# A decoder trunk on one core: the second gate's row requested late in the second product of the down projection, and an eviction's x tiles two steps behind its first operations

## The chip, the cores and the metric

The kernel runs on one core of one Trainium2 chip. The metric is the device time of one execution in microseconds (us). Engines are named as the profile names them: PE is TensorE (PEld its weight loads), DVE VectorE, ACT ScalarE, POOL GpSimd, SP SyncE, which here issues the DMAs (SPq is its queue of them).

## What is computed

One layer of an autoregressive trunk: a modulated RMSNorm, a mixer of three head groups, a gated residual, a second modulated RMSNorm, and a convolutional feed-forward network with a gated residual. The change lies in the last product, `w_down`, and in the gated residual `gt2` behind it. Cut to that:

```python
D_MODEL, SEQ, D_FF = 1024, 2048, 2816

def conv_ffn(h, w_up, w_conv, b_conv, w_down):
    z = h @ w_up
    z = causal_depthwise_conv(z, w_conv, b_conv)
    a, gv = jnp.split(z, 2, axis=-1)
    return (jax.nn.silu(a) * gv) @ w_down

def reference(x, c, ...):
    ...
    x = x + gt1 * y
    h = rms_norm(x, g_ffn[l]) * (1.0 + sc2) + sh2
    x = x + gt2 * conv_ffn(h, w_up[l], w_conv[l], b_conv[l], w_down[l])
    return x
```

All is float32.

## The kernel before

**The down projection.** The activations lie transposed in device memory as `act_d` (2816 x 2048), x after the mixer as `x2_d` (2048 x 1024), the two gates as `gt_d` (2 x 1024). The 2048 positions are done in two halves H of 1024. For each half the product of activations (2816 deep) and `w_down` is cut into 2 x 2 blocks and done with seven block products in place of eight, in the order 1, 2, 7, 6, 5, 4, 3. The sums and differences of blocks that this needs are made on VectorE. Each block product has a depth of 11 slices (`KH`) of 128 rows. A step of the program is one slice of one product: four groups of three matmuls, 12 in all, since each operand is split into a high and a low half to keep float32 precision (`mm3`, L54 high x high, L55, L56). So one half has 77 steps, and every step loads, prepares and multiplies one slice.

**Preparation.** `Down.prep` makes the operands of a slice. For products 1 and 2 they are an activation tile and a weight tile as loaded. For product 7 they are a difference of activations (L1649) and a difference of weight tiles (L1651: the tile `t2w`, minus the freshly loaded `wd`). L1654 and L1655 form product 6's activations. Then both operands are split: ACT copies the high half (L1670, tile `wsph`), VectorE subtracts it to get the low half (L1671, tile `wspl`). These split tiles have 12 buffers, that is three steps. The second matmul of a step is the first to need the low half of the weight tile.

**Loads.** `Down.load` requests the `act` tiles (128 x 1024, 512 KB, L1622) and the weight tiles `wd` and `t2w` (128 x 512, 256 KB, L1628) six steps ahead. `wd` has 8 buffers; a request waits on SyncE's queue until its buffer is free, and whatever is behind it on the queue waits too. The gate row `gt2` (one row of 1024 spread over 128 partitions, 512 KB into the core) is requested once, where the program reaches step `n_left`, which is slice 4 of product 1 in the first half (L2009).

**Eviction.** When a product's sum is complete, `Down.post` puts work on the list `later`; the loop takes one entry at each step. `Down.final` is the eviction of products 2, 5 and 4: per group of 128 rows it requests an x tile (tag `s`, four buffers, L1705), makes a first operation on the sum (L1719: times gate, or L1717: plus a kept sum), and in a later entry finishes (L1724, L1725) and writes the result out (L1726). Product 2 evicts while product 7 runs.

**What sets the order.** From the steps behind the first 14 on, the order of instructions on each engine is not that of the text: the framework's scheduler orders them by priority, by what is ready in its own reckoning, and by the buffers that are free. So a moved request can change the order on engines that the diff does not mention. SyncE, VectorE and ACT each do their instructions in the order that the scheduler left.

The two places in the code:

```python
        if i == n_left:                                  # L1999
            ...
            gt2 = pool.tile([P, D], F32, name="gt2")
            dma(gt2, gt_d[1:2, :].broadcast_to([P, D]))  # L2009
```

Of the kernel before, what the change touches and what calls it, by code (L numbers as in the profile page):

```python
# [33 lines left out]
def trunk(  # L34
# [307 lines left out]
    def h_load(n):  # L342

        out_ = []
        for k in range(4):
            t = b_tile(n, k)
            dma(t.bitcast(F32), hc_d[COMBO.index(n), k])
            out_.append(t)
        return out_
# [8 lines left out]
    def down_open_right():  # L358
        pool.open("dn_r", "right", ("wd", 2048, 8))
        pp.open("dn_r", "right", ("db0", 2048, 4))  # L360
# [261 lines left out]
    class Weights:  # L622
# [7 lines left out]
        def load(self, n=2):  # L630
            k = len(self.raw)
            if k == KT:
                return
            raw = pool.tile([P, 512], F32, name="wr", tag=self.tags[k])
            o = 0
            for col, wd in self.parts[:n]:
                dma(raw[:, o : o + wd], w_in[k * P : (k + 1) * P, col : col + wd])
                o += wd
            self.raw.append(raw[:, : self.width])
# [857 lines left out]
    class Group:  # L1497
# [37 lines left out]
        def prep(self, p):  # L1535
            self.sums(p)
            self.high(p)
            self.low(p)
# [70 lines left out]
    class Down:  # L1609
# [90 lines left out]
        def rest(self, ti, nl, i):  # L1700

            r = slice(self.H * 1024 + ti * 512 + i * P, self.H * 1024 + ti * 512 + i * P + P)
            ns = slice(nl * 512, nl * 512 + 512)
            xr = self.tmp("s")
            dma(xr, x2_d[r, ns])  # L1705
            return r, ns, xr

        def final(self, ti, nl, src, more=None):
            got = {}

            def load(i):
                got[i] = self.rest(ti, nl, i)

            def sum_(i):
                got["o", i] = o = self.tmp("o")
                if more:
                    V.tensor_tensor(o, src[i], more[i], op=ALU.add)  # L1717
                else:
                    V.tensor_tensor(o, src[i], gt2[:, nl * 512 : nl * 512 + 512], op=ALU.mult)  # L1719

            def rest(i):
                (r, ns, xr), o = got[i], got["o", i]
                if more:
                    V.tensor_tensor(o, o, gt2[:, ns], op=ALU.mult)  # L1724
                V.tensor_tensor(o, o, xr, op=ALU.add)  # L1725
                dma(out[r, ns], o)  # L1726

            for i in range(4):
                later.append(lambda i=i: (load(i), sum_(i)))
            for i in range(4):  # L1730
                later.append(lambda i=i: rest(i))

        def post(self, p):
# [38 lines left out]
    def down_open_left():  # L1772
        pool.open(
            "dn_l", "left", ("t2w", 2048, 11), ("s1", 2048, 4), ("u2", 2048, 4), ("o", 2048, 5), ("gt2", 4096, 1), *[("act%d" % n, 4096, 1) for n in range(12, 14)]
        )
        pp.open("dn_l", "left", ("db1", 2048, 4))


    later = []
# [22 lines left out]
    at_ = {s: i for i, s in enumerate(steps)}  # L1802
# [22 lines left out]
    def up_groups(i):  # L1825

        n = len(groups)
        if n < len(gs) and (n < 2 or last_of[gs[n - 2]] <= i):
            groups[gs[n]] = Group(*gs[n])
# [168 lines left out]
    for i, s in enumerate(steps):  # L1998
        if i < 14:  # L1999
            continue  # L2000
        if i == n_left:
            while later:
                later.pop(0)()
            pool.close("up_l")
            pool.close("zy")
            pp.close("up_l")
            down_open_left()
            gt2 = pool.tile([P, D], F32, name="gt2")
            dma(gt2, gt_d[1:2, :].broadcast_to([P, D]))  # L2009
        if i == n_open:  # L2010
            groups[s[1], s[2]].mm(s[3])
        if i == n_open:
            pp.close("up_r")
            down_open_right()
        if i >= n_open:
            while loaded < min(i + AHEAD + 3, n_left + AHEAD + 3 if i < n_left else len(steps)):
                load(loaded)
                loaded += 1
        prep(i + AHEAD)
        if i == 14:  # L2020
            written.close()
        up_groups(i + AHEAD)
        if i != n_open:
            if s[0] == "up":
                groups[s[1], s[2]].mm(s[3])
            else:
                downs[s[1]].mm(s[2], s[3])
        if i:
            q = steps[i - 1]
            if q[0] == "up":  # L2030
                groups[q[1], q[2]].post(q[3])
                if q[1:3] == (0, 21) or q[1:] == (0, 21, 3):
                    hb[1, OF[q[3]]] = h_load(OF[q[3]])
            elif q[3] == KH - 1:
                downs[q[1]].post(q[2])
        if later:
            later.pop(0)()
# [34 lines left out]
```

## Time and profile before

| what | value |
|---|---|
| runs shown | 2573.66, 2574.22, 2579.74 us; median 2574.22 |
| the profiled execution's own time | 2579.28 us |
| its span, from first to last instruction | 2577.6 us |
| granted TensorE clock in it | 0.998 |
| busy: PE, DVE, ACT | 98%, 77%, 50% of the span |
| moved by DMA | 379.57 MB, mean 147 GB/s |
| gate row issued, and first used | 2169.6, 2214.3 us |

A busy share says how full an engine is over the whole span. What a stage is worth is read from that stage's own window. Three views follow each other in the reading: windows that compare stages, an engine's instructions in order of time with what ended its waits in square brackets, and the chain of waits that ended last. A DMA's row in a timeline of SPq is its issue only; that its data has landed shows in the chain, or in who waits for it.

### The profile page before, as it was taken

How to read it: one execution, taken by the hardware profiler on the slowest of the kernel's cores; microseconds unless marked ns; L12 is line 12 of the kernel's file. 1: busy time of each engine (PE TensorE's matmuls, PEld its weight loads, DVE VectorE, ACT ScalarE, POOL GpSimd, SP SyncE). 2: the span in 40 equal slices, each digit the busy share in tenths (PEclk: the TensorE clock that was granted, in tenths of full speed). 3: DMA queues.
4: the chain of work that ended last, by engine and by line, in shares of the span. 5: the costliest groups of instructions: out<-in, count | busy, mean ns of one | idle time of the engine just before them, and what ended most of it. 6: DMA issues, size and time to landing. Idle time of an engine off the chain costs nothing.

```text
span 2577.6 us, 36355 instructions
## 1 busy us (share of the span) xinstructions
PE 2526.7 (98%) x12553; PEld 2099.4 (81%) x12569; DVE 1993.4 (77%) x3406; ACT 1281.9 (50%) x2443; POOL 404.5 (16%) x537
## 2 busy tenths in 40 slices
PE   6999999999999999999999999999999999999999
PEld 6888888888787877778878888888888887888887
DVE  7657656576388888865689888888888887997897
ACT  5443343433388788843555444444444444444443
POOL 2013310133266566510000000000000000000000
PEclk9999999999999999999999999999999999999999
DMA  7345753455654445157823222265222218567423
GB/s 261 111 124 168 220 176 95 132 161 145 181 155 132 119 127 168 54 192 233 294 82 98 89 83 82 83 219 172 90 74 88 85 66 290 184 234 264 155 86 119
DMA packets 302671, 379.57 MB, mean 147 GB/s; under 512 B 31758, under 2 KB 194412, under 8 KB 300440
## 3 DMA queue, kind: packets, MB, share of 16 engines
q1 hardware_dynamic: 302488, 377.26, 46.3%
q8 instruction: 99, 1.62, 0.3%
q14 instruction: 84, 0.69, 0.1%
HBM read 276.44 MB, written 100.74 MB: 146 GB/s over the span
## 4 chain that ended last, share of the span: by engine, by line
PE 54%; DVE 5%; DMA 4%; ACT 2%; issue 2%; POOL 1%; SPq 0%; ACTq 0%; DVEq 0%
PE ub L56 10%; PE ub L55 10%; PE ub L54 10%; PE db L55 5%; PE db L56 5%; PE db L54 5%; PE tp L259 2%; PE sp L206 2%; PE op L245 1%; PE op L246 1%; DMA ld<-y_d 1%; DMA x_d<-x 1%; DMA hc_d<-hl 1%; DMA ld<-yt_d 1%; DVE L L212 1%
## 5 line engine op out<-in xcount | busy, mean ns | idle before, releaser
L54 PE MATMUL acc<-wh,hh 128*128 128x512 f32 (+2 forms) x752 | 280.7, 374 | 1.2 <-DVE vhl L815 1.2
L54 PE MATMUL ub<-T,wsph 128*128 128x512 f32 x704 | 273.9, 389 | 1.2 <-ACT wsph L1529 1.2
L55 PE MATMUL ub<-T,wsph 128*128 128x512 f32 x704 | 274.3, 390 | 0.2 <-DVE T L1477 0.2
L56 PE MATMUL ub<-T,wspl 128*128 128x512 f32 x704 | 273.9, 389 | 0.0
L56 PE MATMUL acc<-wh,hl 128*128 128x512 f32 (+2 forms) x752 | 269.7, 361 | 0.3 <-DVE hl L606 0.2
L55 PE MATMUL acc<-wl,hh 128*128 128x512 f32 (+2 forms) x752 | 269.3, 359 | 0.6 <-DVE wl L648 0.6
L55 PE MATMUL db<-wspl,wsph 128*128 128x512 f32 x616 | 240.0, 390 | 2.6 <-DVE wspl L1671 2.4
L56 PE MATMUL db<-wsph,wspl 128*128 128x512 f32 x616 | 239.5, 389 | 0.0
L54 PE MATMUL db<-wsph 128*128 128x512 f32 x616 | 239.5, 389 | 0.0
L1529 ACT CAST wsph<-S 128x512 fp32r<-128x512 f32 x176 | 109.3, 622 | 219.3 <-PE ub L55 151.9
L263 DVE TENSOR_TENSOR plo<-tp,phi 128x512 fp32r<-128x512 f32 (+1 forms) x320 | 187.0, 607 | 30.9 <-ACT phi L262 29.0
L55 PE MATMUL ub<-B,wsph 128*128 128x512 f32 x528 | 205.7, 390 | 0.9 <-DVE B L1477 0.8
L54 PE MATMUL ub<-B,wsph 128*128 128x512 f32 x528 | 205.7, 390 | 0.0
L56 PE MATMUL ub<-B,wspl 128*128 128x512 f32 x528 | 205.5, 389 | 0.0
L223 ACT ACTIVATE L<-L,nm 128x1024 f32<-128x1024 f32 (+2 forms) x192 | 172.5, 902 | 34.8 <-DVE nm L212 32.7
L259 PE MATMUL tp<-ident,L 128*128 128x128 f32 x1088 | 177.7, 275 | 6.4 <-DVE plo L263 4.0
L262 ACT CAST phi<-tp 128x512 fp32r<-128x512 f32 (+1 forms) x320 | 159.7, 520 | 43.5 <-PE tp L259 41.8
L1670 ACT CAST wsph<-act 128x512 fp32r<-128x512 f32 x132 | 82.3, 624 | 195.1 <-PE db L55 185.0
L206 PE MATMUL sp<-kk,q 128*128 128x512 f32 (+3 forms) x640 | 170.3, 377 | 3.5 <-DVE nm L212 2.5
L228 POOL TENSOR_SCALAR L<-L,rs 128x1024 f32<-128x1024 f32 (+2 forms) x192 | 168.0, 885 | 11.0
L259 PEld LDWEIGHTS tp<-ident,L 128*128 128x128 f32 x1088 | 131.0, 141 | 37.3 <-DVE plo L263 8.5
L56 PEld LDWEIGHTS acc<-wh,hl 128*128 128x128 f32 x752 | 142.4, 190 | 22.0 <-DVE hl L606 0.7
(338 smaller groups left out, 5969.7 us busy)
## 6 DMA issues: line engine op xcount, KB each, us to landing
w<-in_w_up_dram SPq DMA_DIRECT2D x88, 512.0 KB
wd<-in_w_down_dram SPq DMA_DIRECT2D x154, 256.0 KB
wa<-in_w_ada_dram SPq DMA_DIRECT2D x96, 256.0 KB
act_d<-yc SPq DMA_DIRECT2D x44, 512.0 KB
act<-act_d SPq DMA_DIRECT2D x44, 512.0 KB
wr<-in_w_in_dram SPq DMA_DIRECT2D x64, 256.0 KB
q<-q_d SPq DMA_DIRECT2D x128, 128.0 KB
hc_d<-hl SPq DMA_DIRECT2D x28, 512.0 KB
```

Of the source, the lines that this page charges most:

```text
L54: T.matmul(ps, lh, rh, start=start, stop=False, skip_group_check=resume)
L55: T.matmul(ps, lh, rl, start=False, stop=False, skip_group_check=resume)
L56: T.matmul(ps, ll, rh, start=False, stop=stop, skip_group_check=resume)
L206: T.matmul(sp[:, b : b + bw], q2[n][:, qs], kk[:, s0 + b : s0 + b + bw], start=n == 0, stop=n == 1 and not last)
L212: V.tensor_tensor_reduce(out=L[c], in0=sp[:, :w], in1=nf[:, s0 : s0 + w], scale=-1.0, scalar=3.0e38 if c == 0 else nm[:, 0:1], op0=ALU.add ...
L223: A.activation(L[c], L[c], AF.Exp, bias=nm[:, n - 1 : n], scale=-1.0, accum_out=rs[:, c : c + 1])
L228: G.tensor_scalar(t, t, rs[:, 0:1], 1.0, op0=ALU.mult, op1=ALU.mult)
L259: T.transpose(tp[:, i * P : (i + 1) * P], rows[i][j // 8][:, (j % 8) * P : (j % 8 + 1) * P], ident)
L262: A.copy(hi[:, c0:], tp[:, c0:])
L263: V.tensor_tensor(lo[:, c0:], tp[:, c0:], hi[:, c0:].bitcast(F32), op=ALU.subtract)
L1529: A.copy(self.wa[p][0], self.source(p))
L1670: A.copy(hi, v)
```

## The change

The gate row's tile is still made at `n_left`, but its request moves to slice 9 of product 2 in the first half, 16 steps on in the program. In `final`, the request of the x tile of a group moves from the entry of the group's first operation to the entry two steps later, and where it meets a finishing entry it stands behind it. The number of entries stays at 8.

```diff
-            for i in range(4):
-                later.append(lambda i=i: (load(i), sum_(i)))
-            for i in range(4):
+            for i in range(6):
+                later.append(lambda i=i: (i < 4 and sum_(i), i > 3 and rest(i - 4), i > 1 and load(i - 2)))
+            for i in range(2, 4):
                 later.append(lambda i=i: rest(i))
...
             gt2 = pool.tile([P, D], F32, name="gt2")
+        if i == at_["dn", 0, 2, 9]:
             dma(gt2, gt_d[1:2, :].broadcast_to([P, D]))
```

No instruction is added or removed. What the scheduler makes of it shows at three places, all in the first half's products 1, 2 and 7. Elsewhere, and on PE everywhere, the order stands; ACT swaps one copy with one cast. The numbers behind the names count tiles; from the gate row on they are one or a few lower after the change, and otherwise mean the same tiles.

SyncE's queue, where the gate row stood, before:

```order
L1628 DMA wd_21962<-in_w_down_dram 128x512
L1622 DMA act_22096<-act_d_73 128x1024
L2009 DMA gt2_21814<-gt_d_71 128x1024
L1622 DMA act_21888<-act_d_73 128x1024
L1622 DMA act_21912<-act_d_73 128x1024
```

and where it stands now, with the x tiles of product 2's eviction behind it (`wd_22149`, `wd_22173`, `wd_22197` are the weight tiles of slices 0, 1, 2 of product 7, `wd_22308` and `wd_22335` of slices 6 and 7):

```order
L1628 DMA wd_22149<-in_w_down_dram 128x512
L1628 DMA t2w_22195<-in_w_down_dram 128x512
L2010 DMA gt2_21814<-gt_d_71 128x1024
L1628 DMA wd_22173<-in_w_down_dram 128x512
L1628 DMA wd_22197<-in_w_down_dram 128x512
...
L1628 DMA wd_22277<-in_w_down_dram 128x512
L1628 DMA wd_22308<-in_w_down_dram 128x512
L1628 DMA wd_22335<-in_w_down_dram 128x512
L1705 DMA s_22362<-x2_d_70 128x512
L1628 DMA wd_22364<-in_w_down_dram 128x512
```

The gate row moved 19 requests further on; it stood ahead of the activation tile of product 2's slice 1 (`act_21888`), and now stands ahead of the weight tile of product 7's slice 1. The first x tile moved behind two more weight tiles.

VectorE at the end of product 1, before (`act_21840` and `wd_21842` belong to its slice 10, `act_21864` and `wd_21866` to slice 0 of product 2, `act_21888` to slice 1):

```order
L1671 TENSOR_TENSOR wspl_21893<-act_21840,wsph_21892 128x512
L1671 TENSOR_TENSOR wspl_21897<-wd_21842,wsph_21896 128x512
L1654 TENSOR_TENSOR act_21593<-act_21593,act_21888 128x512
L1655 TENSOR_TENSOR act_21593<-act_21593 128x512
L1671 TENSOR_TENSOR wspl_21917<-act_21864,wsph_21916 128x512
L1654 TENSOR_TENSOR act_21610<-act_21610,act_21912 128x512
L1671 TENSOR_TENSOR wspl_21921<-wd_21866,wsph_21920 128x512
```

and now:

```order
L1654 TENSOR_TENSOR act_21593<-act_21593,act_21887 128x512
L1671 TENSOR_TENSOR wspl_21892<-act_21839,wsph_21891 128x512
L1655 TENSOR_TENSOR act_21593<-act_21593 128x512
L1671 TENSOR_TENSOR wspl_21896<-wd_21841,wsph_21895 128x512
L1654 TENSOR_TENSOR act_21610<-act_21610,act_21911 128x512
L1671 TENSOR_TENSOR wspl_21916<-act_21863,wsph_21915 128x512
L1655 TENSOR_TENSOR act_21610<-act_21610 128x512
L1671 TENSOR_TENSOR wspl_21920<-wd_21865,wsph_21919 128x512
```

L1654, which reads the activation tile of product 2's slice 1, moved ahead of both splits of product 1's slice 10.

VectorE in product 2, from the splits of its slice 6 to those of its slice 8, before (`wd_22022`, `wd_22048`, `wd_22074` are the weight tiles of slices 6, 7, 8; the L1651 rows are product 7's, slices 1 to 6):

```order
L1651 TENSOR_TENSOR t2w_22020<-wd_22174,t2w_22020 128x512
L1671 TENSOR_TENSOR wspl_22077<-act_22018,wsph_22076 128x512
L1671 TENSOR_TENSOR wspl_22081<-wd_22022,wsph_22080 128x512
L1651 TENSOR_TENSOR t2w_22046<-wd_22198,t2w_22046 128x512
L1651 TENSOR_TENSOR t2w_22072<-wd_22225,t2w_22072 128x512
L1671 TENSOR_TENSOR wspl_22103<-act_22044,wsph_22102 128x512
L1651 TENSOR_TENSOR t2w_22098<-wd_22252,t2w_22098 128x512
L1671 TENSOR_TENSOR wspl_22107<-wd_22048,wsph_22106 128x512
L1651 TENSOR_TENSOR t2w_22124<-wd_22277,t2w_22124 128x512
L1671 TENSOR_TENSOR wspl_22129<-act_22070,wsph_22128 128x512
L1651 TENSOR_TENSOR t2w_22148<-wd_22310,t2w_22148 128x512
L1671 TENSOR_TENSOR wspl_22133<-wd_22074,wsph_22132 128x512
```

and now, the two pieces that differ:

```order
L1651 TENSOR_TENSOR t2w_22019<-wd_22173,t2w_22019 128x512
L1651 TENSOR_TENSOR t2w_22045<-wd_22197,t2w_22045 128x512
L1671 TENSOR_TENSOR wspl_22076<-act_22017,wsph_22075 128x512
L1671 TENSOR_TENSOR wspl_22080<-wd_22021,wsph_22079 128x512
...
L1651 TENSOR_TENSOR t2w_22123<-wd_22277,t2w_22123 128x512
L1651 TENSOR_TENSOR t2w_22147<-wd_22308,t2w_22147 128x512
L1671 TENSOR_TENSOR wspl_22128<-act_22069,wsph_22127 128x512
L1651 TENSOR_TENSOR t2w_22171<-wd_22335,t2w_22171 128x512
L1671 TENSOR_TENSOR wspl_22132<-wd_22073,wsph_22131 128x512
```

Slice 2's L1651 moved ahead of the splits of product 2's slice 6, and slice 7's ahead of the weight split of its slice 8, where slice 6's stood last before.

## The prediction

> **What bounds the kernel now.** The page's busy shares come first, then the windows of the down projection, since both edits lie there and nowhere else.
>
> ```profile
> PE 2526.7 (98%) x12553; PEld 2099.4 (81%) x12569; DVE 1993.4 (77%) x3406; ACT 1281.9 (50%) x2443; POOL 404.5 (16%) x537
> ...
> core 0: us, PE busy (x) PEld busy (x) DVE busy (x) ACT busy (x) POOL busy (x), PEclk, DMA share, GB/s
> 2147.00:2220.00 73.00, 70.45 (x307) 56.97 (x306) 58.42 (x91) 33.23 (x57) 0.00 (x0) 1.00 0.84 289
> 2220.00:2565.00 345.00, 345.00 (x1524) 285.67 (x1523) 304.86 (x500) 150.60 (x266) 0.00 (x0) 1.00 0.51 170
> 2565.00:2577.60 12.60, 8.01 (x35) 6.14 (x34) 6.83 (x10) 0.72 (x2) 0.00 (x0) 0.97 0.22 83
> ```
>
> TensorE (PE) sets the end. From 2220 to 2565 it has not one idle moment, so nothing done there can save time. In 2147 to 2220, the first two products of the first half, 73.00 - 70.45 = 2.55 us are idle. That is nearly all that this change can reach; the 4.6 us after 2565 are the last eviction, which it does not touch. PE's own rows say where the idle time is:
>
> ```profile
> 2177.88 0.39 PE L55 MATMUL db<-wspl,wsph 128*128 128x512 f32 x1
> ...
> 2180.37 0.39 PE L54 MATMUL db<-wsph 128*128 128x512 f32 x1
> 2181.63 0.50 PE L55 MATMUL db<-wspl,wsph 128*128 128x512 f32 x1 [0.87 <-DVE wspl L1671]
> 2181.97 0.40 PE L56 MATMUL db<-wsph,wspl 128*128 128x512 f32 x1
> ...
> 2184.25 0.39 PE L54 MATMUL db<-wsph 128*128 128x512 f32 x1
> 2184.77 0.50 PE L55 MATMUL db<-wspl,wsph 128*128 128x512 f32 x1
> 2185.10 0.39 PE L56 MATMUL db<-wsph,wspl 128*128 128x512 f32 x1
> ...
> 2198.27 0.39 PE L54 MATMUL db<-wsph 128*128 128x512 f32 x1
> 2198.50 0.39 PE L55 MATMUL db<-wspl,wsph 128*128 128x512 f32 x1
> ...
> 2203.71 0.39 PE L54 MATMUL db<-wsph 128*128 128x512 f32 x1
> 2205.66 0.50 PE L55 MATMUL db<-wspl,wsph 128*128 128x512 f32 x1 [1.56 <-DVE wspl L1671]
> 2206.00 0.40 PE L56 MATMUL db<-wsph,wspl 128*128 128x512 f32 x1
> ```
>
> Undisturbed, a matmul starts every 345.00 / 1524 = 0.226 us, so one slice of a product, 12 matmuls, takes 2.72 us. Against that spacing the delays, each with the matmul behind it, are 1.14 us at slice 0 of the second product (2180.37), 0.39 us at slice 1 (2184.25) and 1.83 us at slice 8 (2203.71): 3.36 us, counted by starts. Each time the second matmul lacks the low half of its weight tile, which VectorE writes at L1671. The chain of waits says why VectorE is late, and its timeline shows the queue it holds:
>
> ```profile
> 2169.67 0.30 SPq L2009
> 2170.07 8.25 DMA act<-act_d
> 2189.68 5.61 DMA wd<-in_w_down_dram
> 2198.13 6.09 DMA wd<-in_w_down_dram
> ...
> 2178.35 0.69 DVE L1654 TENSOR_TENSOR act<-act 128x512 f32<-128x512 f32 x1 [4.21 <-DMA act<-act_d]
> 2180.29 0.68 DVE L1654 TENSOR_TENSOR act<-act 128x512 f32<-128x512 f32 x1
> 2180.89 0.69 DVE L1671 TENSOR_TENSOR wspl<-wd,wsph 128x512 fp32r<-128x512 f32 x1
> ...
> 2193.30 0.69 DVE L1651 TENSOR_TENSOR t2w<-wd,t2w 128x512 f32<-128x512 f32 x1 [3.65 <-DMA wd<-in_w_down_dram]
> 2197.12 0.68 DVE L1651 TENSOR_TENSOR t2w<-wd,t2w 128x512 f32<-128x512 f32 x1
> 2202.91 0.69 DVE L1651 TENSOR_TENSOR t2w<-wd,t2w 128x512 f32<-128x512 f32 x1 [2.12 <-DMA wd<-in_w_down_dram]
> 2204.92 0.69 DVE L1671 TENSOR_TENSOR wspl<-wd,wsph 128x512 fp32r<-128x512 f32 x1
> ```
>
> VectorE stands in the preparation of later products (L1654 for product 6, L1651 for product 7), waiting for a transfer, and the splits that PE needs next are behind it. The first wait goes back to an activation tile requested right after the gate row (SPq L2009). So the gate row really is on the path at the first delay. The third delay has nothing of it: x tiles and wd tiles are in flight there.
>
> **The change part by part.** First, the gate row leaves 2169.6. What it held up is read from SyncE's queue and from the DMA windows:
>
> ```profile
> SPq L1628 <- DMA gt<-gt_d: 1.6, 1, 1.6
> ...
> 2176.55 0.33 SPq L1628 DMA_DIRECT2D wd<-in_w_down_dram  x1
> 2194.02 1.53 SPq L1628 DMA_DIRECT2D wd<-in_w_down_dram  x2
> ...
> 2170.00:2182.00 12.00, 11.13 (x50) 8.91 (x49) 6.21 (x10) 6.46 (x14) 0.00 (x0) 1.00 1.00 333
> 2186.00:2194.00 8.00, 8.00 (x37) 6.60 (x36) 4.35 (x9) 3.43 (x6) 0.00 (x0) 1.00 0.97 334
> 2194.00:2195.00 1.00, 1.00 (x6) 0.84 (x5) 1.00 (x2) 0.00 (x0) 0.00 (x0) 1.00 0.41 154
> ```
>
> The queue's 1.6 us wait for the gate row ends at 2176.5: the row landed then, 1.8 us before the activation tile behind it (2170.07 + 8.25 = 2178.3). The engines are full (share 1.00) and serve in order here, so the activation tile takes the gate's place and lands at 2176.5. Unchanged VectorE order would save slices 0 and 1 their 1.14 + 0.39 = 1.53 us. But the order changes: L1654 now stands ahead of the split of slice 10 of the first product. Starts on VectorE are 0.60 us apart (2180.29, 2180.89), so L1654 at 2176.5 is followed by the act split at 2177.1, L1655 at 2177.7 and the wd split at 2178.3, done at 2179.0. PE wants it at 2177.88: a new delay of 1.1, with the matmul behind it 1.2 us. The next slices follow without a wait (wd split of slice 0 at 2180.7, done at 2181.4, wanted at 2181.7). Net: -1.53 + 1.2 = -0.3 us. Bounds: the new delay is 0 if the tile lands as fast as the wd tile (2169.6 + 5.61 = 2175.2), and 3.1 us if it lands at 2178.35 as before. I take 1.2, by the gate's own landing.
>
> Second, the gate row is now requested ahead of the wd tile for slice 1 of product 7, which was issued at 2189.68 and landed 5.61 us later at 2195.3. Its 524,288 bytes take 1.57 us at 334 GB/s, so slice 1 lands at 2196.9. Slice 2 is issued when L1651 of slice 0 has freed a buffer (2193.30 + 0.69, issued 2194.02), and was used at 2197.12, so it takes 3.1 us or less. The engines had 0.59 us of free time in 2194 to 2195; the gate's bytes fill that, and the rest falls on slice 2: between 2197.1 and 2198.7, I take 2197.7. In the new VectorE order both L1651, of slices 1 and 2, stand ahead of the split of slice 6 of the second product. That gives L1651 at 2197.7, the act split at 2198.3, the wd split at 2198.9, done at 2199.6. PE, 0.3 us earlier than before, wants it at 2198.2 instead of 2198.50: a delay of 1.45 us. At slice 8 the wd split now waits for L1651 of slice 7, formerly slice 6. Slice 7's request leaves when slice 3's L1651 (at 2199.5, next after that split) has freed its buffer, at 2200.2, and no longer has two x tiles ahead of it; at 3.1 us plus part of a tile I have it at 2203.8, L1651 at 2204.2, the split at 2204.8, done at 2205.5, where PE at 2199.65 + 2 x 2.72 = 2205.1 waits 0.4 us. The old delay at slice 8, 1.83 us, is replaced by 1.45 + 0.4 = 1.85. Bounds: 0 if slice 2 lands before 2196.3, and 6.3 us if every landing takes the longest measured 6.09 us (worked out with the rivals).
>
> Third, the consumers of the late tiles:
>
> ```profile
> L1719 DVE TENSOR_TENSOR o<-db,gt x8: 681/684/684, 2214.3 to 2427.4; 128x512 f32<-128x512 f32 x8
> L1725 DVE TENSOR_TENSOR o<-o,s x24: 681/684/687, 2222.1 to 2553.4; 128x512 f32<-128x512 f32 x24
> L1705 SPq DMA_DIRECT2D s<-x_d x32: 319/423/1588, 2197.6 to 2527.8; - x32
> ```
>
> The gate is first used at 2214.3. Requested near 2189 and landing after even 8.25 us, it has 17 us to spare. Of the 32 x requests only four change place on SyncE's queue; the first left at 2197.6 and is used at 2222.1, and at 2200.5 it still has some 15 us after 6.09 us of transfer. So both edits cost nothing by lateness; what hides it is PE's work on six further slices. Without that cover each would cost its whole landing, 6 to 8 us.
>
> The sum against the profiled execution's span, 2577.6 us: -1.53 + 1.2 - 1.83 + 1.85 = -0.3 us. The profiled execution took 2579.28 us, 5.1 us above the median of the three runs shown, 2574.22; the terms are differences, so I take them from the median: 2573.9 us.
>
> **The rivals.** B, short landings: with the gate gone the tiles come soon enough that VectorE never keeps PE waiting; all 3.36 us go, and the time is 2570.9 us. For it speaks the second half, which has the same products and no gate row:
>
> ```profile
> 2355.00:2425.00 70.00, 70.00 (x311) 57.95 (x310) 52.45 (x84) 31.69 (x56) 0.00 (x0) 1.00 0.57 187
> ```
>
> PE does not wait there at all. Against it: the engines are busy to 0.57 there and to 0.84 in 2147 to 2220. The Trainium skill, "SBUF — State Buffer", section "The DMA setup-cost knee", would give this rival: it has a transfer take about 2 us plus its bytes at 436 GB/s, an estimate of 2.6 us for a wd tile and 3.2 us for an activation tile. The trace does not agree in this stretch, with 5.61, 6.09 and 8.25 us, since requests queue behind each other.
>
> C, the slower side: L1651 of slice 2 holds VectorE until its tile has landed, with slice 6's split behind it. If that takes the longest time measured for such a tile, 2194.02 + 6.09 = 2200.1, the wd split starts at 2201.3 and is done at 2202.0: 3.8 us late. Slice 7 of product 7, requested when slice 3's L1651 is through near 2202.6, lands at 2208.7, and the split is done at 2210.0 where PE at 2202.0 + 2 x 2.72 = 2207.45 waits 2.5 us. Together 6.3 in place of 1.83, with -0.3: +4.2, so 2578.4 us. It decides as soon as slice 2 lands after about 2198.0; from there each us late is a us of PE. With the first bound too (3.1 for 1.2) it is +6.1, 2580.3 us.
>
> D, the change does less than it says: the gate row is named late in the second product, but the queue has it only some 20 requests further on, while that product's first slices run, and the buffers decide most of the rest. Then the delays only change places: 2574.2 us.
>
> **How the numbers follow.** My forecast, near 2573.9, has 0.45; B 0.22; C 0.25; D 0.08. All four lie within 0.3% of 2574.22 (7.7 us), about what a measurement of this kernel can tell from no change. The range reaches from B, with half a us for its rounding, to C with part of the first bound: 2570.4 to 2580.0. The run spread before, 2573.66 to 2579.74, fits in it. Faster by over 0.3% would need more than the idle time there is, so 0.03, for runs that scatter. Slower by over 0.3% needs C's worst and more, or scatter: 0.10. Within: 0.87.
>
> **What would show it.** The gate's issue moves from 2169.6 to about 2189 and L1654's first wait ends near 2176.5. PE's delays stand at slice 10 of the first product and at slices 6 and 8 of the second, not at slices 0 and 1. If all are gone, B is right; if L1651's wait ahead of slice 6 is over 2 us longer than I have it, C. PE idle after 2220, or L1719 or L1725 waiting for a DMA, would prove the third part wrong, and a change over 7.7 us the whole.

## The result, and the profile after

| | before, in the same runs | after the change |
|---|---|---|
| median of 17 runs each | 2575.5 us (2572.84 to 2581.36) | 2580.45 us (2577.44 to 2582.59) |
| ratio, 95% interval | | 1.0015 [1.0009, 1.0022] |
| profiled execution: time, span, clock | 2579.28, 2577.6, 0.998 | 2578.68, 2576.7, 0.997 |

The change makes the kernel slower by 0.15%, 0.0015 x 2575.5 = 3.9 us (2.3 to 5.7 by the interval). That is less than 0.3%, but the interval does not reach 1. The two medians are 4.95 us apart; this text goes by the ratio, which has the interval. The two profiled spans can't be subtracted: in the profile of before, what lies ahead happened to run later. The first matmul of product 1's slice 10 starts 3.43 us later there than after the change, where it starts at 2174.22:

```profile
2177.65 0.39 PE L54 MATMUL db<-wsph 128*128 128x512 f32 x1
```

So the stage is compared with itself, and a time of the changed kernel "in the frame of before" is that time plus 3.43 us. The windows of the changed kernel, columns as before:

```profile
2147.00:2220.00 73.00, 69.91 (x294) 55.49 (x293) 57.45 (x89) 33.19 (x56) 0.00 (x0) 0.98 0.79 277
2206.00:2208.00 2.00, 2.00 (x6) 1.56 (x7) 2.00 (x4) 0.00 (x0) 0.00 (x0) 0.59 0.99 363
2208.00:2210.00 2.00, 2.00 (x7) 1.57 (x6) 2.00 (x4) 0.00 (x0) 0.00 (x0) 0.56 1.00 364
2220.00:2565.00 345.00, 345.00 (x1524) 285.65 (x1523) 303.16 (x498) 151.10 (x266) 0.00 (x0) 1.00 0.52 170
```

PE is still without a gap from 2220 on. In the stage of the change it is idle for 73.00 - 69.91 = 3.09 us, where it was 2.55, and for some 3.6 us it has another loss that idle time does not show: the granted clock (the column behind the engines) is 0.59 and 0.56, and only 6 or 7 matmuls start in 2 us, where nearly 9 fit. PE's rows show both:

```profile
2174.22 0.39 PE L54 MATMUL db<-wsph 128*128 128x512 f32 x1
2175.14 0.50 PE L55 MATMUL db<-wspl,wsph 128*128 128x512 f32 x1 [0.54 <-DVE wspl L1671]
...
2194.09 0.39 PE L54 MATMUL db<-wsph 128*128 128x512 f32 x1
2194.68 0.50 PE L55 MATMUL db<-wspl,wsph 128*128 128x512 f32 x1 [0.20 <-DVE wspl L1671]
...
2197.33 0.39 PE L54 MATMUL db<-wsph 128*128 128x512 f32 x1
2198.09 0.50 PE L55 MATMUL db<-wspl,wsph 128*128 128x512 f32 x1 [0.38 <-DVE wspl L1671]
...
2203.77 0.39 PE L54 MATMUL db<-wsph 128*128 128x512 f32 x1
2205.92 0.50 PE L55 MATMUL db<-wspl,wsph 128*128 128x512 f32 x1 [1.76 <-DVE wspl L1671]
...
2206.60 0.63 PE L54 MATMUL db<-wsph 128*128 128x512 f32 x1
2207.03 0.63 PE L55 MATMUL db<-wspl,wsph 128*128 128x512 f32 x1
```

These are slice 10 of product 1 and slices 6, 7 and 9 of product 2. Each time the second matmul of a slice lacks the low half of its weight tile, as before, but at other slices. Against the undisturbed spacing of 0.226 us the delays, each with the matmul behind it, are 0.80, 0.46, 0.64 and 2.03 us (and 0.24 at slice 8). Slices 0 and 1 have none now. Behind the longest, seven matmuls in a row start 0.43 us after the one ahead of them; with the shorter steps at both ends that adds 1.6 us.

The chain of waits and VectorE's timeline say what VectorE stood at:

```profile
2166.16 6.41 DMA act<-act_d
...
2198.36 6.19 DMA wd<-in_w_down_dram
```

```profile
2172.59 0.69 DVE L1654 TENSOR_TENSOR act<-act 128x512 f32<-128x512 f32 x1 [4.62 <-DMA act<-act_d]
2173.20 0.69 DVE L1671 TENSOR_TENSOR wspl<-act,wsph 128x512 fp32r<-128x512 f32 x1
2173.80 0.69 DVE L1655 TENSOR_TENSOR act<-act 128x512 f32<-128x512 f32 x1
2174.41 0.68 DVE L1671 TENSOR_TENSOR wspl<-wd,wsph 128x512 fp32r<-128x512 f32 x1
...
2191.85 0.69 DVE L1651 TENSOR_TENSOR t2w<-wd,t2w 128x512 f32<-128x512 f32 x1 [0.72 <-DMA wd<-in_w_down_dram]
2192.73 0.69 DVE L1651 TENSOR_TENSOR t2w<-wd,t2w 128x512 f32<-128x512 f32 x1 [0.19 <-DMA wd<-in_w_down_dram]
...
2203.23 0.69 DVE L1651 TENSOR_TENSOR t2w<-wd,t2w 128x512 f32<-128x512 f32 x1 [2.18 <-DMA wd<-in_w_down_dram]
2203.84 0.68 DVE L1671 TENSOR_TENSOR wspl<-act,wsph 128x512 fp32r<-128x512 f32 x1
2204.57 0.69 DVE L1651 TENSOR_TENSOR t2w<-wd,t2w 128x512 f32<-128x512 f32 x1
2205.18 0.68 DVE L1671 TENSOR_TENSOR wspl<-wd,wsph 128x512 fp32r<-128x512 f32 x1
```

First, L1654 waits 4.62 us for the activation tile of slice 1 of product 2, and the weight split of slice 10 (2174.41) stands third behind it. Last, L1651 of slice 8 of product 7 waits 2.18 us, and between it and the weight split of slice 9 (2205.18) stands L1651 of slice 9 too. SyncE's queue has the weight tiles of those two slices between the x tiles:

```profile
2184.15 0.44 SPq L2010 DMA_DIRECT2D gt<-gt_d  x1
...
2196.56 0.43 SPq L1705 DMA_DIRECT2D s<-x_d  x1
2197.47 0.33 SPq L1628 DMA_DIRECT2D wd<-in_w_down_dram  x1
2197.84 0.42 SPq L1705 DMA_DIRECT2D s<-x_d  x1
2198.36 0.38 SPq L1628 DMA_DIRECT2D wd<-in_w_down_dram  x1
```

Before, the first x tile stood two weight tiles earlier, between those of slices 5 and 6. The wait of 2.12 us at 2202.91 there was slice 5's L1651, the one behind it slice 6's, and the split that came too late was that of slice 8. Now they are slices 8 and 9, and the split is that of slice 9.

The order of VectorE in the section on the change stops at the splits of slice 8. Behind them it differs too. Before, slice 8's L1651 (2206.93) stood between the two splits of slice 9, and slice 9's (2208.28) behind both:

```profile
2205.59 0.69 DVE L1651 TENSOR_TENSOR t2w<-wd,t2w 128x512 f32<-128x512 f32 x1
2206.20 0.68 DVE L1671 TENSOR_TENSOR wspl<-act,wsph 128x512 fp32r<-128x512 f32 x1
2206.93 0.69 DVE L1651 TENSOR_TENSOR t2w<-wd,t2w 128x512 f32<-128x512 f32 x1
2207.54 0.68 DVE L1671 TENSOR_TENSOR wspl<-wd,wsph 128x512 fp32r<-128x512 f32 x1
2208.28 0.69 DVE L1651 TENSOR_TENSOR t2w<-wd,t2w 128x512 f32<-128x512 f32 x1
```

Now both stand one place further ahead, as the rows from 2203.23 to 2205.18 show. So slice 9's weight split now waits for the tiles of slices 8 and 9, where it waited for those of slices 7 and 8.

### The profile page after: what moved, and what is told of

Read it like the earlier page. It is cut to its first block, busy times and chain, and to the rows that moved or that the text cites. A ratio compares the mean times of both kernels' runs of the same rounds, so it can differ in the third digit from the quotient of the medians.

```text
span 2576.7 us, 36369 instructions
## 1 busy us (share of the span) xinstructions
PE 2528.1 (98%) x12569; PEld 2099.3 (81%) x12569; DVE 1993.7 (77%) x3406; ACT 1282.7 (50%) x2443; POOL 406.3 (16%) x537
## 4 chain that ended last, share of the span: by engine, by line
PE 53%; DVE 5%; DMA 5%; ACT 2%; issue 2%; POOL 1%; SPq 0%; ACTq 0%; DVEq 0%
PE ub L56 10%; PE ub L55 10%; PE ub L54 10%; PE db L55 5%; PE db L56 5%; PE db L54 5%; PE tp L259 2%; PE sp L206 2%; PE op L245 1%; PE op L246 1%; DMA ld<-y_d 1%; DMA ld<-yt_d 1%; DMA x_d<-x 1%; DMA hc_d<-hl 1%; DVE L L212 1%
```

## The experiments

Fifteen runs, 11 timed executions each, in four groups; every ratio is against the kernel before in the same group on the same chip (medians there 2575.98, 2576.25, 2576.51 and 2573.63 us). The theories named in the expectations: O says that the moved order on VectorE is the cause, since an instruction that waits for a tile holds up the splits behind it. G says that it is the bytes of the gate row at their new place, X that it is the x tiles at theirs. P came last: that the late requests are worth something by themselves, hidden by the order.

Delays of PE are sums of start-to-start times beyond 0.226 us over both products, half-speed matmuls included, from the one profiled execution of each run. With the original two profiles:

| kernel | ratio, 95% interval | delays, us | where (p1, p2: product; slice) |
|---|---|---|---|
| before, profile shown | | 3.65 | p2: 0, 1, 8 |
| before again | 0.9994 [0.9985, 1.0002] | 2.41 | p2: 0, 1, 7 to 10 |
| after | 1.0015 [1.0009, 1.0022] | 6.48 | p1: 5, 10; p2: 6 to 9; half speed |
| after again | 1.0015 [1.0006, 1.0024] | 3.94 | p1: 10; p2: 6 to 9 |
| gate row late alone | 1.0010 [1.0001, 1.0019] | 4.08 | p1: 10; p2: 6, 8 to 10 |
| x tiles late alone | 1.0005 [0.9996, 1.0014] | 2.85 | p2: 0, 1, 8, 9 |
| no gate row | 1.0008 [0.9999, 1.0017] | 5.75 | p1: 5, 10; half speed; p2: 9 |
| changed requests, old VectorE order | 0.9998 [0.9989, 1.0007] | 1.05 | p2: 7, 9, 10 |
| changed, L1654 alone put back | 1.0003 [0.9994, 1.0012] | 1.98 | p2: 9 |
| changed, L1651 alone put back | 1.0004 [0.9995, 1.0013] | 2.13 | p2: 7, 9 |
| changed, both held later | 0.9988 [0.9979, 0.9997] | 0.00 | |
| the same, repeated | 0.9992 [0.9983, 1.0001] | 0.00 | |
| gate row late, both held later | 0.9991 [0.9982, 1.0000] | 0.11 | |
| kernel before, both held later | 0.9990 [0.9981, 0.9999] | 0.49 | p1: 5, 6 |
| x tiles late, both held later | 0.9995 [0.9986, 1.0004] | 0.00 | |
| written order, requests of before | 1.0003 [0.9994, 1.0012] | 2.16 | p2: 0, behind ACT |
| written order, changed requests | 1.0004 [0.9994, 1.0013] | 1.76 | p2: 0, behind ACT |

**The two kernels as they are.** No edit.

> The kernel before once more, for a second profile: both theories have the delays at slices 0, 1 and 8 of product 2 again, 2.5 to 4 us in sum, and a ratio to before of 1 within its interval. Half-speed matmuls in this stretch here too would mean that they are not the change's alone.

> The changed kernel once more, for a second profile and a second timing. Both theories: +3 to +5 us against before; PE delays at slice 10 of product 1 and slices 6 to 9 of product 2, 4 to 5 us in sum. If the half-speed matmuls behind slice 9 belong to these delays and not to one execution, they are there again, some 2 us more.

The change's 1.0015 came again. In the repeat there is no stretch of low clock, though the wait at slice 9 is nearly as long:

```profile
2203.91 0.39 PE L54 MATMUL db<-wsph 128*128 128x512 f32 x1
2205.84 0.50 PE L55 MATMUL db<-wspl,wsph 128*128 128x512 f32 x1 [1.54 <-DVE wspl L1671]
```

So the half speed is an extra of some executions. The repeat of before had 0.4 and 0.34 us at slices 0 and 1 of product 2, not the 1.14 and 0.39 us from which the prediction worked, and at slice 8 0.4 in place of 1.83. Slices 7, 9 and 10, which had lost nothing, lost 0.2, 0.5 and 0.5. One profiled execution had sized these terms. The sum, 2.41, is just below the 2.5 to 4 expected.

**One part of the change alone.** The two hunks of the change, each by itself: the gate row's request at slice 9 of product 2, and the x tiles two entries later.

> The gate row is requested at slice 9 of product 2 as in the change; the x tiles are requested as before. Theory G (the gate row's new place ahead of the wd tiles of product 7, with two L1651 ahead of slice 6's splits, is what costs): PE delays at slice 10 of product 1 near 0.8 us and at slices 6 and 7 of product 2 near 0.5 us each, as in the changed kernel, and the old delay of 1.8 us at slice 8, since the x tiles stand where they stood; delays 1 us or more above before's 3.4 us in sum, time +2 to +5 us against before. Theory X (the x tiles' new place costs): delays at slices 0 and 1 gone, nothing new but 0.8 us at slice 10, time -1 to 0 us.

> The x tiles are requested two steps behind the first operations; the gate row is requested as before. Theory G: the delay of 1.8 us at slice 8 of product 2 moves to slice 9 with about its old length, the delays of 1.5 us at slices 0 and 1 stay; time within 1.5 us of before. Theory X: the delay at slices 8 and 9 grows by 2 us or more, time +2 to +5 us.

The parts also part the order. The gate row alone moves L1654 and slice 2's L1651 ahead, as in the change; the x tiles alone move slice 7's L1651, and behind it those of slices 8 to 10, one place ahead. With the gate row alone the delay at slice 10 of product 1 is 1.19 us and that at slice 6 is 1.64; slice 8 has 0.76, where G had expected the old 1.8. With the x tiles alone, slices 0 and 1 keep theirs (0.70 and 0.40), and the delay of slice 8 turns up at slice 9, with the same cause:

```profile
2203.71 0.39 PE L54 MATMUL db<-wsph 128*128 128x512 f32 x1
2205.24 0.50 PE L55 MATMUL db<-wspl,wsph 128*128 128x512 f32 x1 [1.14 <-DVE wspl L1671]
```

By time the gate row's part is clear of 1 and that of the x tiles can't be told from nothing; but the two intervals overlap, so the shares stay open.

**No gate row at all.** The gate's tile is filled with ones on GpSimd, so the last residual leaves its second gate out, and the row is not requested at all. The x tiles stay early in the text; on SyncE's queue two of them leave earlier than before, behind the weight tiles of slices 2 and 3, and two behind those of slices 7 and 8. VectorE's order in products 1 and 2 comes out as in the change.

```diff
-            dma(gt2, gt_d[1:2, :].broadcast_to([P, D]))
+            G.memset(gt2, 1.0)
```

> The gate row is not loaded: its tile is filled with ones on GpSimd, so the second gate is left out of the result; x tiles as before. It bounds what any place for the gate row can bring. Theory G: the delays at slices 0, 1 of product 2 (1.5 us) fall to 0.5 or less and none is new at slices 6 and 7; slice 8 keeps its delay or loses up to 1.8 us; time -1 to -3.4 us against before. Theory X says the same of the gate row, so this run sizes the gate's share for both.

By time it lies between the two kernels, and the interval parts it from neither; G had expected it 1 to 3.4 us below before. By the trace, the delay at slice 10 does not need the gate row. Without a byte of it L1654 waits longer than before, since in the new order VectorE comes to it earlier, with both of slice 10's splits still to do:

```profile
2170.40 0.69 DVE L1671 TENSOR_TENSOR wspl<-wd,wsph 128x512 fp32r<-128x512 f32 x1
2177.00 0.69 DVE L1654 TENSOR_TENSOR act<-act 128x512 f32<-128x512 f32 x1 [5.91 <-DMA act<-act_d]
2177.61 0.69 DVE L1671 TENSOR_TENSOR wspl<-act,wsph 128x512 fp32r<-128x512 f32 x1
2178.21 0.69 DVE L1655 TENSOR_TENSOR act<-act 128x512 f32<-128x512 f32 x1
2178.81 0.69 DVE L1671 TENSOR_TENSOR wspl<-wd,wsph 128x512 fp32r<-128x512 f32 x1
```

The delay at slice 10 is 2.10 us, the longest seen there, and half speed follows it (the granted clock is the third number from the right):

```profile
2178.00:2180.00 2.00, 0.45 (x2) 0.40 (x3) 2.00 (x4) 0.44 (x1) 0.00 (x0) 1.00 0.78 298
2180.00:2182.00 2.00, 2.00 (x7) 1.57 (x6) 2.00 (x5) 1.08 (x2) 0.00 (x0) 0.58 0.71 239
2182.00:2184.00 2.00, 2.00 (x6) 1.54 (x6) 2.00 (x4) 1.04 (x3) 0.00 (x0) 0.57 0.72 225
```

Slices 6 and 7 have no delay here, as G expected. But the delay at slice 10 and the half speed behind it bring PE there some 3.6 us later, which leaves VectorE that much more time, so this run does not decide between G and O at these two slices. Slice 9 has 1.60 us.

**The changed requests in the old order.** L1654 and L1651 of the first half are held behind those splits behind which they stood before the change (`issue_after` only orders instructions on one engine; it adds no wait for data). PE's work is the change's, and SyncE's requests too, but for one swap of an activation and a weight tile. VectorE's order is that of before, but for the weight split of product 2's slice 1, which stays one place earlier, as in the change. In all kernels with holds the line numbers go up: L1651 is L1654 there, L1654 is L1659, and the split L1671 is L1676.

```diff
+                after = {1: (2, 5, 1), 2: (2, 6, 1), 6: (2, 8, 0), 7: (2, 8, 1), 8: (2, 9, 0), 9: (2, 9, 1), 10: (2, 10, 0)}.get(k)
+                with tc.issue_after(self.split_[after]) if after and self.H == 0 else ExitStack():
-                V.tensor_tensor(bv, B[0], bv, op=ALU.subtract)
+                    V.tensor_tensor(bv, B[0], bv, op=ALU.subtract)
...
+                after = {1: (1, 10, 1), 2: (2, 0, 0)}.get(k)
+                with tc.issue_after(self.split_[after]) if after and self.H == 0 else ExitStack():
-                V.tensor_tensor(a(2, 1), a(2, 1), a(2, 2), op=ALU.add)
+                    V.tensor_tensor(a(2, 1), a(2, 1), a(2, 2), op=ALU.add)
```

A key (2, 5, 1) means product 2, slice 5, weight tile; 0 is the activation tile.

> All requests of the changed kernel, but L1654 and L1651 are held behind the splits that stood ahead of them before the change. Theory O (the new order on VectorE costs, since a wait for a tile stands ahead of splits that PE needs sooner; the gate row's transfer costs little): the delay at slice 10 of product 1 is gone or moves to slice 0 of product 2 with under 0.8 us, those at slices 6 and 7 fall under 0.3 us each; delays at least 1 us less in sum than in the changed kernel, time -1 to +1.5 us against before. Theory G (the gate row's bytes ahead of product 7's tiles cost): slices 6 to 9 keep 2 us or more of delay, time +2 to +5 us.

This is the run that decides: late requests, old order, and the loss is gone (0.9998). Against the change's 1.0015 only the order differs, up to that swap. The reverse, the new order with all the old requests, was not run; the kernel without the gate row comes nearest to it, and its time settles nothing.

**Written order.** The stretch from `n_left` to slice 2 of product 7 in the order of the text, with the requests of before and of the change.

```diff
+            written.enter_context(tc.manual_schedule())
+        if i == at_["dn", 0, 7, 2]:
+            written.close()
+        if i == n_left:
```

> The kernel before with the order of the text, on every engine, from slice 4 of product 1 to slice 2 of product 7 in the first half: no L1654 and no L1651 stands ahead of a split that PE needs sooner. The gate row is requested at slice 4 of product 1. Theory O: no PE delay over 0.5 us in product 2, time -1 to -4 us against before. Theory G: the gate row ahead of the activation tile still delays the start of product 2 by 0.8 us or more; the rest is gone.

> The changed kernel with the order of the text over the same steps. Theory O: the same as written_before within 1 us, since without waits ahead of the splits neither place of the gate row is felt. Theory G: 1.5 us or more slower than written_before, with delays at slices 6 to 9 of product 2.

Ratios 1.0003 [0.9994, 1.0012] and 1.0004 [0.9994, 1.0013]: where the scheduler has no say, early and late requests take the same time, which again speaks against G and X. O had expected 1 to 4 us less than before here and no delay over 0.5 us in product 2, and missed both. As a test of O it says less, since the text's order brings a wait of its own, for the copies that empty product 1's sums:

```profile
2179.21 0.39 PE L56 MATMUL db<-wsph,wspl 128*128 128x512 f32 x1
2181.49 0.50 PE L54 MATMUL db<-wsph 128*128 128x512 f32 x1 [1.89 <-ACT s L1697]
```

**One hold at a time.** The two holds of the old order, each alone; the diff is one of the two pieces above.

> The changed kernel with one thing put back: L1654 (product 6's activations) stands on VectorE where it stood before the change, behind the splits of slice 10 of product 1; L1651 stays in the change's order. O (VectorE's order is the cause, in two places): the delay at slice 10 of product 1 (0.57 and 0.80 us in the two profiles of the changed kernel) goes, those at slices 6 to 9 of product 2 stay at 2 to 3.5 us together; ratio 1.0005 to 1.0012. If L1651's order is the whole cause: as the changed kernel, 1.0015. Rival G (the bytes of the gate row at their new place): 1.0015 too, with the delay at slice 10 still there.

> The changed kernel with the other thing put back: L1651 (product 7's weight differences) stands on VectorE where it stood before the change; L1654 stays in the change's order. O: the delay at slice 10 of product 1 stays at 0.5 to 1.2 us, those at slices 6 to 9 of product 2 fall from 2.9 to 3.4 us to 0.8 to 2; ratio 1.0002 to 1.0009. If L1654's order is the whole cause: 1.0015, with L1651's part at nothing. Rival G: 1.0015, the delays at slices 6 to 9 unchanged.

With L1654 put back the delay at slice 10 is gone and slice 9 keeps 1.89 us; with L1651 put back slices 7 and 9 have 1.00 and 1.12, together just above the 0.8 to 2 expected. Slice 9's 1.12 is there though only slice 8's L1651, which waits 1.73 us, stands between its two splits; so putting the order back takes away only a part of that delay, while a late tile still costs the rest. Each brings the ratio down by about 0.0011, both together by 0.0017; with intervals of 0.0009 to each side the shares can't be told apart, and the first ratio came out just below what O had expected. One expectation missed clearly: with L1654 still ahead there was no delay at slice 10. Its tile landed in time in that execution:

```profile
2170.58 0.69 DVE L1659 TENSOR_TENSOR act<-act 128x512 f32<-128x512 f32 x1 [3.82 <-DMA act<-act_d]
```

VectorE then reaches slice 10's weight split at 2172.40. So L1654's place is a risk that costs 0 to 2.1 us from run to run, not a fixed price.

**Holding them later than ever.** L1651 and L1654 stand so far back that a late tile has no split behind it that PE needs soon.

```diff
+                after = (2, min(10, 5 + (k + 1) // 2), 1)
...
+                after = {1: (2, 1, 1), 2: (2, 2, 1)}.get(k)
```

> The changed requests, and in the first half L1654 of slices 1 and 2 behind the weight splits of slices 1 and 2 of product 2, L1651 of slice k behind the weight split of slice 5 + (k + 1) // 2 of product 2 (10 at most): later than before the change and than after it, so that a late tile finds no split behind it that PE needs soon. O: delays in products 1 and 2 together under 1 us, time 1 to 3 us below before, ratio 0.9988 to 0.9997. If L1651 is held too far, product 7's first slices are late instead: 1.5 us or more at its slices 0 to 4 and no gain, 1.0000 to 1.0010. Rival G: 1.0010 to 1.0015, as the requests are the change's.

> The same holds of L1654 and L1651, the gate row late as in the change, the x tiles where they were before it. O: within 0.0005 of the run with the same holds and the late x tiles, since a tile that lands late holds no split up. Rival X (the x tiles at their old place delay product 7's weight tiles): slower than that run by 0.5 to 1.5 us, with a delay of 0.5 to 1.5 us at slices 8 to 10 of product 2.

Every delay is gone, by the row of these matmuls on the page of the changed kernel, and of it with the holds (the last number is PE's idle time ahead of them):

```profile
L55 PE MATMUL db<-wspl,wsph 128*128 128x512 f32 x616 | 240.9, 391 | 3.1 <-DVE wspl L1671 3.1
```

```profile
L55 PE MATMUL db<-wspl,wsph 128*128 128x512 f32 x616 | 239.5, 389 | 0.0
```

VectorE still waits over a us for one of them:

```profile
2199.29 1.43 DVE L1654 TENSOR_TENSOR t2w<-wd,t2w 128x512 f32<-128x512 f32 x2 [1.05 <-DMA wd<-in_w_down_dram]
```

The time falls below that of the kernel before, and early x tiles make no difference beyond the intervals. Their place differs less here than without the holds: the first two leave behind the weight tiles of slices 3 and 6 either way, the other two behind those of slices 7 and 8 or of 9 and 10.

**The requests at one order.** With the holds, PE, VectorE and ACT have the same order with early and with late x tiles, and, apart from one swap on ACT and the numbers of tiles, with an early and a late gate row too. What is left is SyncE's queue.

> The requests of the kernel before (gate row early, x tiles early) with the holds of L1654 and L1651 that brought 0.9988 to the changed requests. PE's and VectorE's instructions then stand in the same order with either set of requests, and only SyncE's queue differs. O (the holds are the gain, the requests are worth next to nothing): ratio 0.9985 to 0.9994, within 1 us of the changed requests with the holds, no delay of PE over 0.3 us in products 1 and 2. Rival P (the late requests are worth something once VectorE doesn't hide it): 1 to 2.5 us slower than the changed requests with the holds, with delays at slices 0 and 1 of product 2, where the gate row's landing decided before.

> The same holds, gate row early, x tiles late. O: as the two others with holds, 0.9985 to 0.9994. Rival P with the x tiles as the part that helps: as the changed requests with the holds, and 1 us or more below early x tiles.

> The changed requests with the holds once more, on the same chip as the two others: 0.9983 to 0.9993, and no delay of PE over 0.3 us in products 1 and 2.

All requests early, only the x tiles late, and both late come out at 0.9990, 0.9995 (just above the 0.9994 expected) and 0.9992, within each other's intervals. Nothing is left for P: slices 0 and 1 of product 2 have no delay even with the gate row where it always was.

```profile
2150.00:2225.00 75.00, 74.97 (x331) 61.46 (x330) 65.28 (x104) 34.63 (x61) 0.00 (x0) 1.00 0.82 282
```

That is the window of the kernel before with the holds: 0.03 us idle. It needs neither part of the change and is faster than the kernel before, at 2571.43 against 2573.63 us; the changed kernel as it is was not timed in this group.

## Why the prediction was wrong in sign, and where it was right

**The bound.** Right: PE sets the end, has no gap after 2220 (345.00 of 345 again), and only the idle time of the first two products could move. Removing all of it brought 0.9988 to 0.9995, on the side of rival B's 2570.9, though by another way than B's.

**First term, -1.53 + 1.2.** The mechanism was right. L1654's wait was to end at 2176.5 in the frame of before; it ended at 2172.59, which is 2176.02 in that frame. The delays of slices 0 and 1 went, and a new one stood at slice 10: 0.80 us, 0.57 in the repeat, 1.19 with the gate row alone. Both sizes hung on one execution: the repeat of before had 0.74 us to lose at slices 0 and 1, not 1.53. That the gate row ahead of this tile makes it late fits the chains of waits: from request to landing the tile took 8.25, 7.52 and 8.00 us in the profiles of before, before again and the x tiles alone, which have the row ahead of it, and 6.01 to 7.70 us in the six whose chain shows it without the row. But the delay at slice 10 comes from L1654's new place, and is there without any gate row.

**Second term, -1.83 + 1.85: the step that failed.** "The old delay at slice 8, 1.83 us, is replaced by 1.45 + 0.4": it was not replaced, it moved. The prediction followed slice 7's tile, which "no longer has two x tiles ahead of it", and that was right: slice 7's L1651 (2199.76) found its tile there. But it stopped at that tile. Slice 9's weight split, for which it put no wait at all, now had slice 9's L1651 ahead of it as well as slice 8's, since both had moved one place ahead, and their tiles, between the x tiles on SyncE's queue, came late. There lie 2.03 and 1.80 us in the two profiles, 1.41 with the x tiles alone, and 1.89 with L1654 put back. The new delays ahead of it were mis-sized too: slice 2's tile was in use at 2192.73 (2196.16 in the frame of before), not at 2197.7, and slice 6 cost 0.46 us, not 1.45 (1.64 with the gate row alone); slice 7, for which nothing was forecast, cost 0.64, and slice 8 0.24, not 0.4. Together 3.4 us in place of 1.85. In the repeats of the two kernels it is 3.4 us in place of 1.7. So the term came to +1.5 and +1.7 us, where the sum has +0.02. That the x tiles themselves make the tiles behind them late is not shown: before, slice 5's tile, requested ahead of all x tiles, came as late (a wait of 2.12 us, against 2.18 for slice 8's now), and with the holds the place of the x tiles made no difference.

**Low clock.** Not foreseen: 1.6 us in one of two profiles.

**Third part, late consumers.** Right. The gate left at 2184.15, against 2189 - 3.43 = 2185.6, and no wait stands ahead of its first use or of the x tiles':

```profile
L1719 DVE TENSOR_TENSOR o<-db,gt x8: 682/684/685, 2211.4 to 2426.5; 128x512 f32<-128x512 f32 x8
its engine sat idle before it (us, times) until:
who waited for it (us, times):
```

**The rivals and the range.** C had the right side and the right mechanism, L1651 holding VectorE, but at slice 2's tile instead of those of slices 8 and 9; that its price, 4.2, is near the measured 3.9 is chance. B's short landings did not come, and D's 2574.2 missed the loss. The measured 2580.45 lies 0.45 above the top of the range. The baseline alone is 1.3 us higher, 2575.5 in that comparison against 2574.22; by the ratio the change would stand at 2578.1 on the median that was used, inside the range, but 4.2 us above the forecast. "Within 0.3%" held.

**What stays open.** In the two profiles of each kernel the delays differ by (6.48 + 3.94) / 2 - (3.65 + 2.41) / 2 = 2.2 us, and the time outside the span by 0.3 (mean 1.94 against 1.65 us in the second pair). The rest of the 3.9 us, about 1.4, is in no row; it is less than the interval is wide. How often the clock drops was not measured.

## What to carry to other kernels

On an engine that does its instructions in a fixed order, as VectorE here, ask of each instruction that waits for a transfer what stands behind it: the price of a late tile is the first thing behind it that the bound engine needs, and moving a request by a few places moves that price to the next victim, it does not take it away. A moved DMA request can reorder other engines through the scheduler, and here the loss went when the old order was put back; test for it by holding the old order with the new requests. And take a delay's size from more than one execution: the same kernel lost 1.53 us at one place in one profile and 0.74 in the next.

## What the runs showed that was not expected

A wait of PE of about 2 us was followed by some 3.6 us at a granted clock of 0.56 to 0.59, in two profiles: behind gaps of 1.92 us (after) and 1.99 us (no gate row) beyond the usual spacing. It was not there behind 1.70 (after again), 1.72 (before), 1.78 (L1654 put back) and 2.05 us (written order, whose row is shown above). So the length of the gap alone does not decide it in these runs; what does is not known from them.
